# Where the right-hand tiles of a hybrid decoder layer begin: 64-byte steps in place of 32 past one

## The chip, the cores and the metric

The kernel runs on one core of one Trainium2 chip. The metric is the device time of one execution in microseconds (us). Three executions of the kernel before gave a median of 1153.29 us, from 1152.1 to 1153.56. A further execution was taken with the hardware profiler; every row of a profile below is from it.

## The reference, cut to what matters

One layer of a decoder on 1024 tokens of width 1024, all in float32:

```python
u = rms_norm(h, norm1_g)                       # (1024, 1024)
proj = u @ w_in                                # 3 x 512 for attention, 4 x 512 for the recurrence
attn = rms_norm(dilated_attention(aq, ak, av)) # 8 heads of 64, three dilations in one softmax
rec = hgrn2_mixer(hq, hf, hi, lb)              # 4 heads of 128, a gated linear recurrence in chunks
rec = rms_norm(rec) * silu(hg)
h = h + concat(attn, rec) @ w_out
u = rms_norm(h, norm2_g)
gate, val = split(u @ w_up)                    # 2 x 2816
h = h + (gelu(causal_conv3(gate)) * val) @ w_down
return rms_norm(h, final_norm_g)
```

## The kernel before, in words

**Products.** A float32 matrix product is made from three TensorE products. Each operand is split into a high part, rounded to the type fp32r, and a low part, what is left (`hi`, `lo`, on ScalarE and VectorE: the casts of line 88 and the subtractions of line 90 for the weights). The function `three` (lines 492 to 494) issues high by high, high by low and low by high into one PSUM bank; `prod` (lines 1233 to 1235) and the loop at lines 1532 to 1534 do the same in the channel mixer. Nearly all these matmuls have a stationary operand of 128x128 and a moving one of 128x512: a row of 2 KB in each partition. A smaller number of matmuls, in the attention and the recurrence and for sums over a row, work on plain float32 tiles, mostly 128x128 and smaller.

**Stages.** (1) The values of the attention and of the recurrence, V and I (PSUM tiles `v` and `i`), from the input x. Here x is the stationary operand and the weights move. (2) Queries and keys, and the recurrence's gates: `pair_block` computes a pair of heads with seven block products (PSUM tile `w`), in which the weights are stationary and x moves. These products also fill the gaps of the attention and of the recurrence, which are written out as steps: `scores`, `turn` and `values` of the attention, `recur` of the recurrence. The last pair of heads goes plainly (`phf`, `phq`). (3) The output projection (`po`). (4) The channel mixer: `w_up` (PSUM tiles `p0g`, `p0v`, `p1g`, `p1v` for the first two groups of columns, then `p`), the convolution, and `w_down` (`ds`, `da`, and `pdl` for the first two blocks of rows).

**Order.** The order of TensorE's instructions is the program's. That of the other engines is laid out by the framework's planner, apart from the instructions that the program pins. The weights go through a ring of five raw and five split buffers (`Ring`, pool `ring`).

**Where the tiles lie.** The on-chip memory (SBUF) is filled from two sides. Pools on the left stand one behind the other from its beginning; pools on the right are stacked from its end downwards, so each right-hand pool begins where the size of those above it puts it. A pool that is closed gives its room to the next.

| side | pools | tiles that matter here |
|---|---|---|
| left | `const`, `ring` | `vec`, `ones`, `lb`; the weights `raww`, `whi`, `wlo` |
| left | `ua` | x and its block sums T1, T3 and B22 for stages 1 and 2 |
| left | `hres`, `op`, `u20`, `u21` | h; the channel mixer's moving operands `b1`, `b12`, `b22`, T1 to T3 of stage 4 |
| left | `dx`, `dw`, `df`, `tail` | the operands of `w_down`: `fhi`, `flo`, `whi`, `wlo` |
| right | `eps` | the first right-hand pool: two constants, open all through |
| right | `ub` | x and its block sums B11, B21, T2 and T4 for stages 1 and 2; later in the same buffers (function `spare`) the operands `attn0`, `attn1`, `rec0`, `rec1` of `po` |
| right | `rv`, `at`, `xp`, `ab` | the identity for transposes; the attention's tiles |
| right | `hg` | the recurrence's tiles |
| right | `ff` | ten buffers of the channel mixer's activations (`atile`); also the split weights `ahiw`, `alow` of one block (stationary) and the split activations `ahi`, `alo` that `pdl` moves |

Tiles of 2 KB to 8 KB and the small ones of 64 bytes keep whatever place within 64 bytes the pool's start gave them. The names T1 to T4 and `whi`, `wlo` occur in two stages; in stages 1 and 2 the names are T1h, T1l and so on in rows of lines 492 to 494, in stage 4 in rows of lines 1233 to 1235.

The code that the diff touches, with the lines of the profile:

Of the kernel before, what the change touches and what calls it, by code (L numbers as in the profile page):

```python
# [10 lines left out]
F32 = mybir.dt.float32  # L11
# [6 lines left out]
P = 128  # L18
# [6 lines left out]
NG = 4  # L25
# [225 lines left out]
def hybrid_kernel(ctx: ExitStack, tc: tile.TileContext, xT, w_qk, w_tok, w_hg, w_out, w_up,  # L251
# [5 lines left out]
    def pool(name, side, **kw):  # L257
        return tc.tile_pool(name=name, bufs=1, side=side, reuse_waits="tile", **kw)
# [9 lines left out]

    lb = cpool.tile([P, 16], F32, name="lb")
    epool = ctx.enter_context(pool("eps", "right"))  # L270
    eps_ = epool.tile([P, 16], F32, name="eps")
    epst, onehalf = eps_[:, 0:1], eps_[:, 8:9]
    ub_cm = pool("ub", "right")
    ub = ub_cm.__enter__()
# [543 lines left out]
    with pool("hg", "right") as hg:  # L818
# [3 lines left out]
        def ht(tag, nm, bufs=1):  # L822
            return hg.tile([P, H2], F32, tag=tag, name=nm, bufs=bufs)
# [98 lines left out]


        lg = vec[:, V_LB : V_LB + 2 * NG]
        tm = hg.tile([P, NG], F32, name="lb_m")
        e01 = hg.tile([P, 2 * NG], F32, name="lb_e")
        DVE.tensor_tensor(tm, lg[:, 0:NG], lg[:, NG : 2 * NG], op=ALU.max)
        DVE.tensor_sub(e01[:, 0:NG], lg[:, 0:NG], tm)
        DVE.tensor_sub(e01[:, NG : 2 * NG], lg[:, NG : 2 * NG], tm)
# [23 lines left out]
        def recur(h, hf):  # L953
            A, E = (gate[h, hf].pop(x) for x in "AE")
            nm = f"{h}_{hf}"
# [6 lines left out]
            C = ht("C", "C" + nm)  # L962
            C3 = C.rearrange("p (c t) -> p c t", c=4)
            DVE.tensor_tensor_scan(C, chunks, A, 0.0, op0=ALU.mult, op1=ALU.add)
            ex = hg.tile([P, 12], F32, tag="ex", name=f"ex{nm}", bufs=2)
            order = tc.keep_in_program_order if (h, hf) == (3, 1) else lambda ins: ins
            A3 = A.rearrange("p (c t) -> p c t", c=4)
            DVE.tensor_sub(A3, C3, C3[:, :, 63:64].to_broadcast([P, 4, P]))
# [48 lines left out]
            for c in range(4):  # L1017
# [2 lines left out]
                PE.matmul(psO[:, s], AT[:, c], iv[:, c], start=True, stop=no_state)  # L1020
                if not no_state:
                    PE.matmul(psO[:, s], E[:, s], st[:, c], start=False, stop=True)
            sq, ss = ht("rs_m", f"hsq{nm}"), hg.tile([P, 12], F32, tag="sm", name=f"hss{nm}", bufs=2)
            for c in range(4):
                s = slice(c * P, (c + 1) * P)
                ACT.activation(sq[:, s], psO[:, s], AF.Square, accum_out=ss[:, c : c + 1])
# [37 lines left out]
        def rec_steps(h, hf):  # L1064
            chain = iter(())

            def first():
                nonlocal chain
                chain = recur(h, hf)
                next(chain)  # L1070

            yield first
            while True:
                yield lambda: next(chain, None)
# [559 lines left out]
```

## Time and profile before

| | |
|---|---|
| median of three executions | 1153.29 us (1152.1 to 1153.56) |
| profiled execution, its own time | 1153.45 us |
| its span, first to last instruction | 1151.7 us |
| mean granted clock of TensorE | 0.998 |
| TensorE matmul (PE) busy | 1138.9 us, 99% of the span, 6412 instructions |
| TensorE weight load (PEld) busy | 929.6 us, 81% |
| VectorE (DVE) busy | 960.3 us, 83% |
| ScalarE (ACT) busy | 586.8 us, 51% |
| GpSimd (POOL) busy | 87.8 us, 8% |
| DMA | 129.84 MB, mean 113 GB/s |

How to read the rows: `L493 PE MATMUL w<-T1l,whi` is the matmul of line 493 that writes the PSUM tile `w`; behind the arrow stands first the operand that moves, then the stationary one. Buffer numbers are left out. The time of a matmul in a row is from its start to its modelled end; matmuls overlap, so the next one begins before the end of the last, and "PE busy" holds such overlaps. The distance from one start to the next is the time that a matmul really takes of TensorE.

### The profile page before, as it was taken

The numbers are of one execution on the slowest core, as the hardware profiler recorded it, in microseconds if no ns is written. First come the engines' busy times: TensorE is split into PE (matmuls) and PEld (weight loads), VectorE is DVE, ScalarE is ACT, GpSimd is POOL, SyncE is SP. The second block draws the span as 40 slices with busy tenths as digits, with TensorE's granted clock in tenths as the row PEclk, the third lists the DMA queues.
The fourth block names the chain that finished last, engine by engine and source line by source line (L and its number), as shares of the span: only waits on it lengthen the run. The fifth ranks groups of instructions, "written<-read, shape, count | busy, mean of one in ns | idle before, by whom it ended". The sixth has DMA issues, their size and how long they took to land.

```text
span 1151.7 us, 17921 instructions
## 1 busy us (share of the span) xinstructions
PE 1138.9 (99%) x6412; PEld 929.6 (81%) x6412; DVE 960.3 (83%) x1748; ACT 586.8 (51%) x1177; POOL 87.8 (8%) x107
## 2 busy tenths in 40 slices
PE   9999999999999999999999999999999999999996
PEld 7887777778888888878788888888888888888885
DVE  7685877768999975889989989888988789857987
ACT  6444455556688875555434434343434354444553
POOL 5210233330000002000000000000000000000000
PEclk9999999999999999999999999999999999999999
DMA  7134222224313543321232233323332387435532
GB/s 249 46 111 145 61 72 62 84 82 159 110 56 110 156 128 103 99 65 38 72 116 98 92 118 125 105 73 111 128 103 80 111 269 230 123 101 171 158 118 75
DMA packets 98633, 129.84 MB, mean 113 GB/s; under 512 B 25008, under 2 KB 44240, under 8 KB 98544
## 3 DMA queue, kind: packets, MB, share of 16 engines
q1 hardware_dynamic: 84256, 104.03, 29.6%
q10 hardware_dynamic: 14288, 24.67, 5.7%
q8 instruction: 50, 0.82, 0.3%
q14 instruction: 39, 0.32, 0.1%
HBM read 97.58 MB, written 31.09 MB: 112 GB/s over the span
## 4 chain that ended last, share of the span: by engine, by line
PE 94%; DVE 3%; ACT 1%; DMA 1%; issue 0%; SPq 0%; ACTq 0%; DVEq 0%
PE p L1235 11%; PE p L1234 11%; PE p L1233 11%; PE w L492 5%; PE w L493 4%; PE w L494 4%; PE ds L1532 3%; PE ds L1533 3%; PE ds L1534 3%; PE po L492 3%; PE po L493 3%; PE po L494 2%; PE da L1533 2%; PE da L1532 2%; PE da L1534 2%; PE S L705 2%
## 5 line engine op out<-in xcount | busy, mean ns | idle before, releaser
L88 ACT CAST whi<-raww 128x512 fp32r<-128x512 f32 x257 | 157.6, 618 | 224.4 <-PE p L1234 78.1
L90 DVE TENSOR_TENSOR wlo<-raww,whi 128x512 fp32r<-128x512 f32 x258 | 179.7, 699 | 33.1 <-ACT whi L88 31.3
L88 ACT CAST whi<-r 128x512 fp32r<-128x512 f32 x70 | 43.6, 623 | 84.8 <-PE ds L1533 48.7
L90 DVE TENSOR_TENSOR wlo<-r,whi 128x512 fp32r<-128x512 f32 x70 | 47.8, 684 | 19.2 <-ACT whi L88 18.3
L1532 PE MATMUL ds<-fhi,whi 128*128 128x512 f32 x160 | 62.3, 389 | 0.0
L1533 PE MATMUL ds<-flo,whi 128*128 128x512 f32 x160 | 62.3, 389 | 0.0
L1534 PE MATMUL ds<-fhi,wlo 128*128 128x512 f32 x160 | 62.2, 389 | 0.0
L1233 PE MATMUL p<-b1h,whi 128*128 128x512 f32 x160 | 62.2, 389 | 0.0
L1234 PE MATMUL p<-b1l,whi 128*128 128x512 f32 x160 | 62.2, 389 | 0.0
L1235 PE MATMUL p<-b1h,wlo 128*128 128x512 f32 x160 | 62.2, 389 | 0.0
L718 POOL TENSOR_SCALAR P<-P,st 128x128 f32<-128x128 f32 (+7 forms) x64 | 45.5, 716 | 103.3 <-DVE st L717 94.4
L1506 POOL TENSOR_TENSOR facc<-facc,sqf 128x256 f32<-128x256 f32 x2 | 1.5, 738 | 674.4 <-ACT sqf L1505 674.4
L90 DVE TENSOR_TENSOR flo<-rawf,fhi 128x512 fp32r<-128x512 f32 x70 | 47.8, 683 | 3.2 <-ACT fhi L88 3.2
L88 ACT CAST fhi<-rawf 128x512 fp32r<-128x512 f32 x70 | 43.1, 616 | 13.5 <-PE p L1235 5.0
L716 ACT ACTIVATE P<-P,st 128x128 f32<-128x128 f32 (+7 forms) x64 | 35.7, 558 | 28.0 <-DVE st L714 28.0
L1262 ACT ACTIVATE cv<-cv 128x512 f32<-128x512 f32 x44 | 27.8, 632 | 40.3 <-DVE cv L1255 40.3
L1255 DVE SCALAR_TENSOR_TENSOR cv<-g,vec,cv 128x511 f32<-128x511 f32 (+2 forms) x92 | 44.6, 490 | 3.6 <-ACT cv L1252 3.3
L1532 PE MATMUL da<-fhi,whi 128*128 128x512 f32 x120 | 46.7, 389 | 0.0
L1533 PE MATMUL da<-flo,whi 128*128 128x512 f32 x120 | 46.7, 389 | 0.0
L1534 PE MATMUL da<-fhi,wlo 128*128 128x512 f32 x120 | 46.7, 389 | 0.0
L714 DVE CUSTOM_DVE_ANT_0 P<-S,mask 128x128 f32<-128x128 f32 (+7 forms) x64 | 28.9, 487 | 8.3 <-PE S L707 6.9
L1534 PEld LDWEIGHTS ds<-fhi,wlo 128*128 128x128 f32 x160 | 30.0, 188 | 6.3
(622 smaller groups left out, 3414.3 us busy)
## 6 DMA issues: line engine op xcount, KB each, us to landing
raww<-in_w_up_dram SPq DMA_DIRECT2D x88, 256.0 KB, 2.9
rawf<-spT SPq DMA_DIRECT2D x40, 256.0 KB, 2.8
r<-in_w_down_dram SPq DMA_DIRECT2D x40, 256.0 KB, 3.5
spB<-a ACTq DMA_DIRECT2D x30, 256.0 KB, 2.2
spT<-t ACTq DMA_DIRECT2D x30, 256.0 KB, 2.1
rawf<-spB SPq DMA_DIRECT2D x30, 256.0 KB, 2.7
raww<-in_w_out_dram SPq DMA_DIRECT2D x28, 256.0 KB, 2.8
raww<-in_w_hg_dram SPq DMA_DIRECT2D x24, 256.0 KB, 2.6
```

The source lines that it names most:

```text
L88: self.pin(self.high(hi[:, :w], raw))
L90: self.pin(low.tensor_sub(lo[:, :w], raw, f32(hi[:, :w])))
L492: PE.matmul(ps, a[0], b[0], start=start, stop=False)
L493: PE.matmul(ps, a[0], b[1], start=False, stop=False)
L494: PE.matmul(ps, a[1], b[0], start=False, stop=stop)
L718: POOL.tensor_scalar(Pt[:, :n], Pt[:, :n], st[:, 3:4], 1.0, op0=ALU.mult, op1=ALU.mult)
L1233: PE.matmul(ps, hi[:, s], bhi, start=(start and n == 0), stop=False)
L1234: PE.matmul(ps, hi[:, s], blo, start=False, stop=False)
L1235: PE.matmul(ps, lo[:, s], bhi, start=False, stop=(stop and n == len(rhs) - 1))
L1532: PE.matmul(ps[d], hi[:, s], ahi, start=(k == 0), stop=False)
L1533: PE.matmul(ps[d], hi[:, s], alo, start=False, stop=False)
L1534: PE.matmul(ps[d], lo[:, s], ahi, start=False, stop=(k == NPAIR - 1))
```

## The change

The constants' tile in the pool `eps` becomes 24 columns wide instead of 16 (96 bytes instead of 64 in each partition); the columns used, 0 to 15, stay the same. Four kinds of small tiles in the pool `hg` become 16 columns wide (64 bytes): `lb_m` (was 4), `lb_e` (was 8), `ex` and `hss` (were 12, two buffers each). The instructions use the same columns of them as before. All right-hand pools stand below `eps`, so their tiles begin 32 bytes lower; they begin at multiples of 64 bytes, where before they began 32 bytes past one.

```diff
@@ -268,7 +268,7 @@
     epool = ctx.enter_context(pool("eps", "right"))
-    eps_ = epool.tile([P, 16], F32, name="eps")
+    eps_ = epool.tile([P, 24], F32, name="eps")
     epst, onehalf = eps_[:, 0:1], eps_[:, 8:9]
@@ -922,8 +922,8 @@
         lg = vec[:, V_LB : V_LB + 2 * NG]
-        tm = hg.tile([P, NG], F32, name="lb_m")
-        e01 = hg.tile([P, 2 * NG], F32, name="lb_e")
+        tm = hg.tile([P, 16], F32, name="lb_m")[:, 0:NG]
+        e01 = hg.tile([P, 16], F32, name="lb_e")[:, 0 : 2 * NG]
@@ -962,7 +962,7 @@
-            ex = hg.tile([P, 12], F32, tag="ex", name=f"ex{nm}", bufs=2)
+            ex = hg.tile([P, 16], F32, tag="ex", name=f"ex{nm}", bufs=2)
@@ -1020,7 +1020,7 @@
-            sq, ss = ht("rs_m", f"hsq{nm}"), hg.tile([P, 12], F32, tag="sm", name=f"hss{nm}", bufs=2)
+            sq, ss = ht("rs_m", f"hsq{nm}"), hg.tile([P, 16], F32, tag="sm", name=f"hss{nm}", bufs=2)
```

## The prediction

> **What bounds the kernel now.** I read the page first: busy shares, slices, the chain of work that ended last.
>
> ```profile
> span 1151.7 us, 17921 instructions
> PE 1138.9 (99%) x6412; PEld 929.6 (81%) x6412; DVE 960.3 (83%) x1748; ACT 586.8 (51%) x1177; POOL 87.8 (8%) x107
> PE   9999999999999999999999999999999999999996
> PE 94%; DVE 3%; ACT 1%; DMA 1%; issue 0%; SPq 0%; ACTq 0%; DVEq 0%
> ```
>
> TensorE is busy in every slice and makes up 94% of the chain. A matmul's row overlaps the next matmul, though, so "busy" could hide stalls. The view in order of time gives the distance between starts, here in stage 1 and in the channel mixer:
>
> ```profile
> 30.11 0.40 PE L492 MATMUL v<-whi,B21h 128*128 128x512 f32 x1
> 30.34 0.39 PE L493 MATMUL v<-wlo,B21h 128*128 128x512 f32 x1
> ...
> 31.04 0.40 PE L493 MATMUL v<-wlo,B21h 128*128 128x512 f32 x1
> ...
> 600.16 0.39 PE L1235 MATMUL p<-b12h,wlo 128*128 128x512 f32 x1
> 600.38 0.39 PE L1233 MATMUL p<-b12h,whi 128*128 128x512 f32 x1
> ...
> 601.06 0.39 PE L1233 MATMUL p<-b12h,whi 128*128 128x512 f32 x1
> ```
>
> In the first group four starts take 0.93 us (30.11 to 31.04), 0.233 each; in the second four take 0.90 (600.16 to 601.06), 0.225 each. Both streams are dense. The difference lies in the matmuls, and the first stream's stationary operand B21 is a right-hand tile. The rows of one line with minimum, median and maximum show this cleanly:
>
> ```profile
> L493 PE MATMUL w<-B11l,whi x36: 391/396/403, 98.7 to 343.9; 128*128 128x512 f32 x36
> L493 PE MATMUL w<-T1l,whi x36: 387/389/397, 112.8 to 358.3; 128*128 128x512 f32 x36
> L493 PE MATMUL w<-T4l,whi x36: 392/395/403, 115.5 to 362.7; 128*128 128x512 f32 x36
> L493 PE MATMUL w<-B22l,whi x36: 387/389/398, 118.3 to 365.5; 128*128 128x512 f32 x36
> L493 PE MATMUL po<-attn0l,whi x32: 392/395/403, 394.3 to 436.1; 128*128 128x512 f32 x32
> L493 PE MATMUL po<-rec0l,whi x32: 392/395/403, 438.5 to 464.8; 128*128 128x512 f32 x32
> L493 PE MATMUL v<-wlo,T4h x16: 393/396/397, 10.7 to 29.6; 128*128 128x512 f32 x16
> L493 PE MATMUL v<-wlo,B22h x16: 389/389/389, 33.1 to 51.7; 128*128 128x512 f32 x16
> ```
>
> Same line, same stage, same weights, same shape: T1 and B22, on the left, have a median of 389 ns; B11, T4, `attn0` and `rec0`, on the right, 395 to 396. In stage 1, where x is stationary, the step is the same: 389 with B22, 396 with T4. So a right-hand operand on either side of the matmul costs about 6.5 ns (395.5 less 389).
>
> Is it the side or the start within 64 bytes? Stage 4 tells:
>
> ```profile
> L1235 PE MATMUL p<-T3h,wlo x80: 389/389/390, 555.8 to 917.7; 128*128 128x512 f32 x80
> L1234 PE MATMUL p1g<-b1l,ahiw 128*128 128x512 f32 x4 | 1.6, 395 | 0.0
> L1234 PE MATMUL p1g<-b1l,whi 128*128 128x512 f32 x4 | 1.6, 389 | 0.0
> L1463 PE MATMUL pdl<-ahi,w 128*128 128x512 f32 x16 | 6.3, 396 | 0.0
> ```
>
> The left pools of stage 4 hold 30 KB of ring, 32 of h, 12 of `op`, 32 of `u20` and 80 of `u21`, whose last tile is T3: it lies where `ub` lay earlier, and still takes 389. The stationary `ahiw` and the moving `ahi` in the right-hand pool `ff` take 395 and 396. High addresses are thus not slow; tiles of right-hand pools are, and what these share is the start 32 bytes past a multiple of 64.
>
> **The change part by part.** No instruction is added, removed or moved, none gets another shape, no transfer or wait is added; the wider tiles are used in the same columns. All that can change is what an access to a right-hand tile costs.
>
> *Matmuls of 512 columns.* With a moving right-hand operand: `w` with B11, B21, T2 and T4, 12 groups of 36, is 432; `po` with four operands, 12 groups of 32, is 384; `phf` and `phq`, 18 groups of 4, are 72; `pdl`, 3 groups of 16, are 48: 936. With a stationary one: `v` and `i` with B11, B21 and T4, 18 groups of 16, are 288; `ahiw` and `alow`, 6 groups of 4, are 24: 312. At 6.5 ns this is 6.1 and 2.0 us, together **8.1 us**.
>
> The 2.0 us rest on the stationary rows alone. The Trainium skill, page "TensorE: Matmul & The Clock Gate", Part 2, step 1, says that loading the next weights takes no read bandwidth from the running matmul, since the two have ports of their own. A reader who goes by that would give hidden weight loads no price and get 6.1 us in place of 8.1. The rows of T4h and B22h disagree: 396 against 389 with the same moving weights.
>
> *Matmuls of 256 columns and plain float32.*
>
> ```profile
> L1463 PE MATMUL pdl<-ahi,w 128*128 128x256 f32 x32 | 9.0, 281 | 0.0
> L372 PE MATMUL ssf<-facchi,ones 128*128 128x256 f32 x1 | 0.3, 282 | 0.0
> L1478 PE MATMUL ssf<-facc,ones x8: 378/379/483, 1139.8 to 1141.9; 128*128 128x256 f32 x8
> L458 PE MATMUL ss<-sums,ones 128*128 128x512 f32 x4 | 1.9, 592 | 0.0
> L733 PE MATMUL Tn<-ident,P 128*128 128x128 f32 x120 | 18.7, 275 | 0.0
> L997 PE MATMUL psU<-iv,kT 128*128 128x128 f32 x56 | 7.5, 274 | 0.0
> ```
>
> At 256 columns the right (`pdl`) takes 281 and the left (`facchi`) 282: nothing to gain in the other 96 matmuls of `pdl`. In plain float32, 512 moving right-hand columns take 592 and 256 left-hand ones 379: 213 ns for 256 columns. Going down the same slope, 128 columns would take 379 - 107 = 272, and the right-hand `psU` and `Tn` show 274 and 275. So I price them at zero; the upper end is 3 ns on some 420 such matmuls that follow one another (transposes 248, `psU` 56, `psO` 120), 1.3 us. Below zero nothing points.
>
> *Other engines and DMA.*
>
> ```profile
> L868 DVE TENSOR_TENSOR E<-E,R 128x512 f32<-128x512 f32 x4 | 2.7, 683 | 0.0
> L1382 DVE TENSOR_TENSOR v<-p,v 128x512 f32<-128x512 f32 x20 | 13.7, 683 | 2.0 <-PE p L1235 2.0
> L463 ACT CAST T2h<-x 128x512 fp32r<-128x512 f32 x4 | 2.5, 622 | 9.7 <-DVE x L479 6.9 <-DMA vd<-vt 2.8
> L1289 ACT CAST T2h<-uf 128x512 fp32r<-128x512 f32 x4 | 2.5, 620 | 1.2 <-DVE uf L1303 1.2
> ar<-raw SPq DMA_DIRECT2D x8, 256.0 KB, 2.8
> raww<-raw SPq DMA_DIRECT2D x8, 256.0 KB, 2.8
> ```
>
> VectorE takes 683 on a right-hand tile and on a left-hand one; ScalarE 622 and 620; the same DRAM tiles land in 2.8 us in the right-hand `ar` and in the left-hand `raww`. Zero for all three, with 2 ns per ScalarE instruction as the bound, off the path.
>
> *What of the 8.1 us reaches the end.* Where TensorE waits for others, a shorter matmul only lengthens the wait.
>
> ```profile
> 0.00:25.00 25.00, 23.67 (x91) 18.94 (x92) 17.42 (x20) 18.14 (x30) 12.29 (x14) 1.00 0.81 276
> 150.00:175.00 25.00, 25.00 (x332) 19.44 (x328) 17.50 (x51) 12.09 (x32) 7.42 (x12) 1.00 0.25 69
> 300.00:325.00 25.00, 25.00 (x139) 20.74 (x138) 24.74 (x46) 21.09 (x53) 2.16 (x1) 1.00 0.25 78
> 350.00:375.00 25.00, 25.00 (x134) 20.33 (x133) 23.03 (x41) 20.23 (x52) 0.29 (x1) 1.00 0.39 116
> PEld S L705 <- DVE st L717: 0.9, 3, 0.4
> ```
>
> (Columns of the first four rows: length, then busy time of PE, PEld, DVE, ACT and POOL, clock, DMA share, GB/s.) At the start x and the weights come in at 276 GB/s and TensorE waits; of the 91 matmuls there I write off the 48 with B11 in V: 48 by 6.5 ns, 0.3 us. In the attention (125 to 275 us) the longest named wait of the weight queue for another engine is 0.9 us, three times 0.3; shorter filling matmuls may give some of it back as waits: 0.2. In the recurrence VectorE is busy 24.74 of 25 us at 300 and 23.03 at 350, so it has 1 to 8% left; the right-hand matmuls of 512 columns there, counted by their starts, are 264 between 275 and 400 us, about 50 in 25 us, worth 0.3 us or 1.3%. It is late next, and I write off 0.5 us between 275 and 400. Sum: 8.1 - 0.3 - 0.2 - 0.5 = **7.1 us**, nearly all before 510 us, and 0.3 us from `pdl` at the end. The profiled execution took 1153.45 us with a span of 1151.7, close to the median of 1153.29; the span becomes 1144.6 and the median **1146.2**.
>
> **The rivals.**
>
> *No change.* The 6.5 ns come from something else about right-hand pools, and 1153.3 us stays. The Trainium skill, page "SBUF — State Buffer", Specifications (TRN2), gives 16-byte cachelines as what an access crosses; 32 past 64 is a whole number of these, so by that page no row would get shorter and the time would be this rival's. For the rival: no right-hand tile at a multiple of 64 exists in this trace. Against it: T3 at high addresses with 389, and VectorE, ScalarE and DMA, which don't tell the sides apart.
>
> *Moving operands only.* Stationary rows stay at 395: 8.1 - 2.0 = 6.1, less 0.8: 1148.0. Against it only that no other cause for those rows is in sight.
>
> *VectorE takes it back.* The recurrence goes at VectorE's pace and all 264 right-hand matmuls between 275 and 400 us give nothing: 1.7 instead of 0.5 us lost; the attention's, 193 by the same count, give nothing either, 1.3 instead of 0.2. 8.1 - 0.3 - 1.3 - 1.7 = 4.8: 1148.5. The digits of VectorE at 300 us speak for it; that TensorE's starts stay dense there, against.
>
> *More.* The float32 matmuls gain their 1.3 us and nothing is written off: 8.1 + 1.3, 1143.9.
>
> *Slower.* The planner lays out VectorE's queue from the tiles that it is given, four kinds of which change size. If it puts weight subtractions (699 ns each, rows of line 90 that write `wlo`) behind the recurrence's, TensorE starves between 275 and 450 us, as VectorE has no room there. Eleven such late ones, 7.7 us, eat the gain; from fourteen, 9.8 us, the kernel is slower by over 0.2%: 1156.0. Nothing in the diff changes a dependency or an instruction's size, so this is remote.
>
> ```profile
> L90 DVE TENSOR_TENSOR wlo<-raww,whi 128x512 fp32r<-128x512 f32 x258 | 179.7, 699 | 33.1 <-ACT whi L88 31.3 <-PE Tn L733 1.0
> ```
>
> **How the numbers follow.** Forecast 0.72; moving only 0.07; VectorE 0.07; more 0.04; no change 0.07; slower 0.03. What this kernel's measurement can tell from no change is about 0.2%, 2.3 us. Faster: 0.72 + 0.07 + 0.07 + 0.04 = 0.90; same 0.07; slower 0.03. The range goes from the "more" case, 1143.9, to just past the two reduced gains, 1149.0; no change and slower are left out.
>
> **What would show it.** Right: the rows `w<-B11l`, `w<-T4l`, `po<-attn0l`, `v<-wlo,T4h`, `p1g<-b1l,ahiw` and `pdl<-ahi,w` (512) at 389 beside unchanged T1 and B22; `pdl` at 256 columns still 281, `psU` 274, `ss` 592; the channel mixer beginning some 7 us earlier with the same length. Wrong: rows still at 395 (no change); `v` at 395 and `w` at 389 (moving only); rows at 389 with more idle time of the weight queue before 510 us (VectorE); left-hand rows that rise.

## The result, and the profile after

Over 22 executions each, the median went from 1152.22 us (1151.75 to 1153.67) to 1150.94 us (1150.59 to 1152.73): a ratio of 0.9987, 95% interval 0.9981 to 0.9993. The change makes the kernel faster by 1.3 us or 0.1%. The prediction was 1146.2 us, 7 us faster; the measured time lies outside its range, 1143.9 to 1149.0 us. The executions of each kernel fall into two groups some 1.7 us apart (near 1151.9 and 1153.5 us before, near 1150.8 and 1152.5 after); the median of three that the prediction started from and both profiled executions are of the second.

The page of the kernel after: the span, the busy times and the chain of work.

```profile
span 1150.6 us, 17921 instructions
PE 1137.8 (99%) x6412; PEld 930.4 (81%) x6412; DVE 959.7 (83%) x1748; ACT 587.0 (51%) x1177; POOL 88.2 (8%) x107
PE 94%; DVE 4%; ACT 1%; issue 1%; DMA 1%; ACTq 0%; SPq 0%; DVEq 0%
```

The bound is as before. The rows of line 493 that the prediction turned on, with minimum, median and maximum in ns, then first and last start in us (the rows of before stand in the prediction):

```profile
L493 PE MATMUL w<-B11l,whi x36: 389/394/400, 97.3 to 342.7; 128*128 128x512 f32 x36
L493 PE MATMUL w<-T1l,whi x36: 387/390/402, 111.4 to 357.2; 128*128 128x512 f32 x36
L493 PE MATMUL w<-T4l,whi x36: 388/395/399, 114.1 to 361.6; 128*128 128x512 f32 x36
L493 PE MATMUL po<-attn0l,whi x32: 388/394/399, 393.3 to 435.0; 128*128 128x512 f32 x32
```

Moving right-hand operands did not fall to 389. They begin at a multiple of 64 now, and still take 394 to 395 beside 390 for the left-hand T1. The groups of the same kernel in which a right-hand operand is stationary tell another tale (behind the bar the busy time in us and the mean of one in ns):

```profile
L1463 PE MATMUL pdl<-ahi,w 128*128 128x512 f32 x16 | 6.3, 395 | 0.0
L493 PE MATMUL v<-wlo,T4h 128*128 128x512 f32 x16 | 6.3, 394 | 0.0
L492 PE MATMUL v<-whi,T4h 128*128 128x512 f32 x16 | 6.3, 392 | 0.0
L494 PE MATMUL v<-whi,T4l 128*128 128x512 f32 x16 | 6.2, 388 | 0.0
```

With T4 stationary, three matmuls that all took 395 or so before now take 394, 392 and 388. The twelve such groups of V and I with T4 and B21 have a mean of 394.8 ns before and 391.7 after. From start to start, which is what counts, the matmuls of V and I with a right-hand operand take 233.2 ns before and 229.0 after, read from the differences of starts in the two traces. 288 of them by 4.2 ns are 1.2 us: the whole gain. The first-start column puts it in the same place: `w<-B11l` begins at 97.3 us instead of 98.7, 1.4 earlier, and `po<-attn0l` at 393.3 instead of 394.3, 1.0 earlier. Nothing is gained behind stage 1: the span is shorter by 1.1 us.

So the rows spoke against the cause that I had given them, but not for "no change" either. What tells stationary from moving operands?

### The profile page after: what moved, and what is told of

It reads as the page before. It is cut to its first block, busy times and chain, and to the rows that moved or that the text cites. A ratio compares the mean times of both kernels' runs of the same rounds, so it can differ in the third digit from the quotient of the medians.

```text
span 1150.6 us, 17921 instructions
## 1 busy us (share of the span) xinstructions
PE 1137.8 (99%) x6412; PEld 930.4 (81%) x6412; DVE 959.7 (83%) x1748; ACT 587.0 (51%) x1177; POOL 88.2 (8%) x107
## 4 chain that ended last, share of the span: by engine, by line
PE 94%; DVE 4%; ACT 1%; issue 1%; DMA 1%; ACTq 0%; SPq 0%; DVEq 0%
PE p L1235 11%; PE p L1234 11%; PE p L1233 11%; PE w L492 5%; PE w L494 5%; PE w L493 5%; PE ds L1532 3%; PE ds L1533 3%; PE ds L1534 3%; PE da L1532 2%; PE da L1533 2%; PE da L1534 2%; PE po L492 2%; PE po L493 2%; PE po L494 2%; PE S L705 2%
```

## Theories

In the program's allocation all left-hand operands, the ring of weights included, begin 192 bytes past a multiple of 512. Right-hand ones begin 416 past before and 384 past after; their slices are whole multiples of 512 further on. Three theories:

- **Multiple of 64**, the prediction's: a tile that begins 32 past a multiple of 64 is slow.
- **Place**: 192 past 512 is a good place by itself, others are bad.
- **Distance**: each matmul moves one operand while weights are loaded beside it. It is slow when the two begin at different places within some period (512 bytes or less). In the stream of V the load of the next weights starts some 3 ns after a matmul and takes 187 to 188 ns, less than the 227 to 235 ns to the next start, so it runs wholly beside that matmul. Left with left has distance 0. Right moving with left weights has 416 - 192 = 224 before and 192 after, and left moving with right weights the reverse.

## Experiments

Times are medians of several executions where a ratio is given. The others had one execution, which may lie anywhere in the 2 us over which this kernel scatters; there the rows carry the verdict. In the expectations "as after" means the kernel after the change.

### Equal starts

```diff
-    eps_ = epool.tile([P, 24], F32, name="eps")
+    eps_ = epool.tile([P, 72], F32, name="eps")
```

> The constants' tile is 72 columns wide instead of 24 (288 bytes): right-hand tiles begin 192 bytes past a multiple of 512, the same place within 512 bytes as all left-hand operands (before it was 416, after the change 384). Theory 'distance' (a matmul is slow when its moving row and the weights loaded meanwhile begin at different places within 512 bytes): all 1248 right-hand matmuls of 512 columns fall from 395 to 389 ns, in w, po, v, i and pdl, and the time to 1144 to 1146 us, 7 us under before. Theory 'multiple of 64' (the change's own): these tiles begin at a multiple of 64 as after the change, so rows and time are those of after, 1150.9 us. Theory 'place' (192 past 512 is good by itself): as 'distance'.

Measured: 1146.86 us, 0.9958 of before (0.9945 to 0.9972). Rows of line 493:

```profile
L493 PE MATMUL w<-B11l,whi x36: 387/389/398, 95.3 to 339.3; 128*128 128x512 f32 x36
L493 PE MATMUL w<-T1l,whi x36: 387/389/397, 109.2 to 353.6; 128*128 128x512 f32 x36
L493 PE MATMUL po<-attn0l,whi x32: 387/389/396, 389.3 to 430.4; 128*128 128x512 f32 x32
L493 PE MATMUL v<-wlo,T4h x16: 389/389/389, 9.1 to 27.5; 128*128 128x512 f32 x16
```

These tiles begin at multiples of 64 as after the change, yet all rows are at 389. "Multiple of 64" is out as the cause. The time is 5.1 us under the median of before in the same comparison (1151.94), a little short of what was expected.

### Both sides moved

```diff
-    lb = cpool.tile([P, 16], F32, name="lb")
+    lb = cpool.tile([P, 56], F32, name="lb")
-    eps_ = epool.tile([P, 24], F32, name="eps")
+    eps_ = epool.tile([P, 32], F32, name="eps")
```

> The left side moves up by 160 bytes (the tile lb is 56 columns wide), and the constants' tile on the right is 32 columns wide: operands of both sides begin 352 bytes past a multiple of 512, which is 32 past a multiple of 64. Theory 'distance': all matmuls of 512 columns at 389 ns, 1144 to 1146 us. Theory 'multiple of 64': everything now begins 32 past, so the right-hand rows are at 395 to 396 and the left-hand ones rise to it too: some 3100 more matmuls by 6 ns, about 1172 us. Theory 'place': neither side is at 192, so everything is slow, about 1172 us.

Measured: 1146.88 us, 0.9957 of before (0.9945 to 0.997). Groups:

```profile
L1235 PE MATMUL p<-T3h,wlo 128*128 128x512 f32 x80 | 31.1, 389 | 0.0
L493 PE MATMUL w<-B11l,whi 128*128 128x512 f32 x36 | 14.1, 390 | 0.0
L493 PE MATMUL po<-attn0l,whi 128*128 128x512 f32 x32 | 12.5, 389 | 0.0
```

Every operand begins 32 past a multiple of 64, and all matmuls are fast. Neither that start nor the place within 512 costs anything; "place" is out too. The time lies 0.9 us above the 1144 to 1146 that "distance" gave, as with equal starts.

### Weights apart from all other operands

```diff
     ringp = ctx.enter_context(pool("ring", "left"))
+    gap = ctx.enter_context(pool("gap", "left")).tile([P, 48], F32, name="gap")
     ...
     DVE.memset(ones, 1.0)
+    POOL.memset(gap, 0.0)
```

> The kernel after the change, with 192 unused bytes put on the left between the ring of weights and the pools behind it, so that the weights stay at 192 past a multiple of 512 and all other operands, left and right, begin at 384. Every tile begins at a multiple of 64. Theory 'distance': some 3012 matmuls that took 389 ns (w with T1, T3 and B22, and the channel mixer's p, p0, p1, ds and da) now have their moving row 192 from the weights and take about 395, as w with B11 does after the change: 3012 by 6.3 ns, 19 us more than after, 1167 to 1171 us; pdl at 512 columns and the matmuls with ahiw, whose two operands are now both at 384, fall to 389. Theory 'multiple of 64': rows and time of after, 1150.9 us. Theory 'own place of a tile': the time rises too, but pdl stays at 395.

Measured: 1168.5 us, 1.0145 of before (1.0129 to 1.0162). Two lines more make line 1235 the one of high by high, and 1465 the first of `pdl`. Groups:

```profile
L1534 PE MATMUL ds<-fhi,whi 128*128 128x512 f32 x160 | 63.2, 395 | 0.0
L1235 PE MATMUL p<-T3h,whi 128*128 128x512 f32 x80 | 31.6, 396 | 0.0
L495 PE MATMUL w<-T1l,whi 128*128 128x512 f32 x36 | 14.2, 395 | 0.0
L1465 PE MATMUL pdl<-ahi,w 128*128 128x512 f32 x16 | 6.2, 389 | 0.0
L1236 PE MATMUL p1g<-b1l,ahiw 128*128 128x512 f32 x4 | 1.6, 388 | 0.0
L1235 PE MATMUL p1g<-b1h,ahiw 128*128 128x512 f32 x4 | 1.6, 394 | 0.0
```

The channel mixer, fast in every other run, becomes slow with all tiles at multiples of 64, and `pdl`, whose operands are now in step (they begin at the same place within the period), becomes fast, 389 to 390. It costs 1168.5 - 1150.9 = 17.6 us against the kernel after; 19 were expected from 3012 matmuls. The theory of distance forecast the size and the larger exception. The other exception came only in part: the six small groups with `ahiw` and `alow`, in step too, stand at 388 to 394, 391.2 on average, where they had 391.5 after the change. They run in two stretches of twelve matmuls between out-of-step ones, and in each the first six or seven take 387 to 398 ns and the rest 388 or 389. What ran just before a matmul thus counts as well.

### The period: 128, 64, 256, 32 and 96 apart

One edit each, in the kernel after: 40, 56, 64 and 48 columns for the constants' tile instead of 24, and for 256 apart

```diff
-    eps_ = epool.tile([P, 24], F32, name="eps")
-    epst, onehalf = eps_[:, 0:1], eps_[:, 8:9]
+    eps_ = epool.tile([P, 8], F32, name="eps")
+    epst, onehalf = eps_[:, 0:1], eps_[:, 4:5]
...
-    DVE.memset(eps_[:, 0:8], EPS)
-    DVE.memset(eps_[:, 8:16], 1.5)
+    DVE.memset(eps_[:, 0:4], EPS)
+    DVE.memset(eps_[:, 4:8], 1.5)
```

> The constants' tile is 40 columns wide: right-hand tiles begin 320 past a multiple of 512, left-hand ones 192: 128 apart, both at multiples of 64. 'Distance' with a period of 512: rows of w and po still above 389, 392 to 395, time 1148 to 1152 us; with a period of 128: 389 and 1144 to 1146 us. 'Multiple of 64': as after the change, 1150.9 us, w at 395 and v between 388 and 395.

> The constants' tile is 56 columns wide: right-hand tiles begin 256 past a multiple of 512, left-hand ones 192: 64 apart. 'Distance' with a period of 512: w and po between 389 and 395, time 1146 to 1152 us; with a period of 64: 389 and 1144 to 1146 us, but then the change's 192 apart would have been fast already, which it was not. 'Multiple of 64': as after the change, 1150.9 us.

> The kernel after the change with the constants' tile 8 columns wide (32 bytes): right-hand tiles begin 448 past a multiple of 512, left-hand ones 192, so 256 apart, at multiples of 64. If the distance counts with a period of 256 or less: 389 ns everywhere and 1146 to 1147 us as with equal starts. If the period is 512 or more: w and po between 391 and 397, 1148 to 1153 us.

> The kernel after the change with the constants' tile 64 columns wide: right-hand tiles begin 224 past a multiple of 256 of which left-hand ones are 192 past, so the moving row of w and po lies 32 behind the weights' start and that of v and i 32 ahead, the reverse of before. If the price is a function of this distance alone, w and po take what v and i took before, 395 to 396, and v and i what w took, 395 to 396; pdl 395. Time 1151 to 1154 us. Theory 'nearly equal is good enough': 389 to 392 and 1147 to 1149 us.

> The kernel after the change with the constants' tile 48 columns wide: right-hand tiles begin 288 past a multiple of 512, left-hand ones 192, 96 apart. If the price is a function of the distance with a period of 256, w and po lie between what was measured 64 apart (390 to 392) and 128 apart (393 to 394); v and i, 96 the other way, at 395 to 396. Time 1150 to 1153 us.

Groups, each fence one kernel, 128, 64, 256, 32 and 96 apart in this order:

```profile
L493 PE MATMUL po<-attn0l,whi 128*128 128x512 f32 x32 | 12.6, 394 | 0.0
L493 PE MATMUL v<-wlo,T4h 128*128 128x512 f32 x16 | 6.3, 395 | 0.0
```

```profile
L493 PE MATMUL po<-attn0l,whi 128*128 128x512 f32 x32 | 12.5, 390 | 0.0
L493 PE MATMUL v<-wlo,T4h 128*128 128x512 f32 x16 | 6.3, 396 | 0.0
```

```profile
L493 PE MATMUL po<-attn0l,whi 128*128 128x512 f32 x32 | 12.5, 390 | 0.0
L493 PE MATMUL v<-wlo,T4h 128*128 128x512 f32 x16 | 6.2, 389 | 0.0
```

```profile
L493 PE MATMUL po<-attn0l,whi 128*128 128x512 f32 x32 | 12.6, 395 | 0.0
L493 PE MATMUL v<-wlo,T4h 128*128 128x512 f32 x16 | 6.3, 396 | 0.0
```

```profile
L493 PE MATMUL po<-attn0l,whi 128*128 128x512 f32 x32 | 12.7, 396 | 0.0
L493 PE MATMUL v<-wlo,T4h 128*128 128x512 f32 x16 | 6.4, 397 | 0.0
```

The times were 1153.37, 1149.93, 1146.82, 1152.26 and 1152.61 us. At 256 apart everything is as fast as with equal starts, so the period is 256 bytes or a divisor of it; 128 apart is slow, which rules out every smaller divisor. The time at 128 apart came out above the 1148 to 1152 expected; that one execution is within the scatter of before, and its rows are slow like those of before. At 96 apart `po` was expected between the values of 64 and 128 apart, 390 to 394, and took 395: the price doesn't rise evenly with the distance.

With the distance counted as start of the moving operand less start of the weights, within 256 bytes, the means in ns of groups of 512 columns fall on one table (averages of the whole numbers that the rows show). `po` is the mean of the four groups of line 493, where x moves; V and I is that of the twelve groups with T4 and B21, where the weights' buffers move and x is stationary:

| distance | 0 | +32 | +64 | +96 | 128 | -96 | -64 | -32 |
|---|---|---|---|---|---|---|---|---|
| `po` | 389.2 | 395.0 | 390.5 | 395.0 | 394.2 | | 395.5 | 395.5 |
| from | equal starts | 32 apart | 64 apart | 96 apart | 128 apart | | after | before |
| V and I | 389.0 | 394.8 | 391.7 | | 394.9 | 395.9 | 395.9 | 395.5 |
| from | equal starts | before | after | | 128 apart | 96 apart | 64 apart | 32 apart |

Two different stages, with the parts of the two sides exchanged, agree to 1.2 ns wherever both were measured. And the table holds the result of the change: the shift by 32 bytes took V and I from +32 (394.8) to +64 (391.7), the one cheap distance besides 0 among those run, and `po` and `w` from -32 to -64, where both cost 395.5.

### Whose weights

```diff
-        for t in order:
+        for t in order if c < KS else ():
     ...
+        for t in range(KS) if c >= KS else ():
+            for a, x in ((0, 0), (0, 1), (1, 0)):
+                for u in (t, t + KS):
+                    ...
+                    PE.matmul(banks[u], y[:, c % KS, tk], w[x], start=False, ...)
```

> The kernel before, with the matmuls of V and I reordered for the second half of x: a right-hand stationary tile (B21) and a left-hand one (B22) take turns, 96 matmuls of each, same work. It tells whose weights matter, the matmul's own or those loaded while it runs. If the next ones ('distance' between the moving row and the load that runs beside it): rows with B22 rise from 389 to 395 or 396, those with B21 fall from 395 to 389 to 391. If a matmul's own weights matter: B21 stays at 395 and B22 at 389. Time within 1 us of before either way.

Measured: 1155.0 us in one execution. Rows of V, taking turns:

```profile
L551 PE MATMUL v<-wlo,B22h x16: 396/396/397, 29.1 to 50.1; 128*128 128x512 f32 x16
L551 PE MATMUL v<-wlo,B21h x16: 394/394/395, 28.9 to 49.9; 128*128 128x512 f32 x16
```

B22, whose own weights are in step and whose next ones are not, rose from 389 to 396: the load that runs beside a matmul counts, as "distance" has it. B21 fell only to 394, not to the 389 to 391 expected, though the load beside it is in step. From start to start the two take 231.7 and 234.9 ns, as much together as two matmuls in a stream that is out of step throughout (233.2 each): taking turns saves nothing.

The trace before holds the same two cases, wherever a stretch with left-hand weights meets one with right-hand weights:

```profile
514.09 0.40 PE L1235 MATMUL p1g<-b1h,wlo 128*128 128x512 f32 x1
514.09 0.19 PEld L1233 LDWEIGHTS p1g<-b1h,ahiw 128*128 128x128 f32 x1
...
516.89 0.39 PE L1235 MATMUL p1g<-b1h,alow 128*128 128x512 f32 x1
516.89 0.19 PEld L1233 LDWEIGHTS p1g<-b12h,whi 128*128 128x128 f32 x1
```

The first of these matmuls has both operands on the left, and the load beside it is right-hand: it takes 396 ns. All 13 matmuls of that kind in V, I and `p1g` do. The second has right-hand weights of its own, and the load beside it is left-hand: it takes 389. Of the 15 of that kind, 5 take 389 and 10 take 393 or 394. So the load that runs beside the matmul counts each time, and a smaller part depends on what ran before. What carries that part over is not shown; the load's rows, 187 to 188 ns in all of this, don't show where the time goes.

The time missed its "within 1 us" by one or two. Of that, 96 rows of B22 by 7 ns explain 0.7. Paired start by start with the trace before, 2.6 us are lost between 98 and 111 us, behind the reordered matmuls: TensorE was busy 3.19 of the 5 us from 105 on (4.08 before) at a granted clock of 0.81 (1.00 before).

### The constants' tile alone

Only the first hunk of the change.

> Only the first part of the change: the constants' tile is 24 columns wide, the four small tiles of the pool hg stay as before. All theories: rows as after the change (w and po 395, v and i between 388 and 395), 1150 to 1153 us; the four small tiles are then worth nothing by themselves. If they matter, rows of the recurrence (psU, psO) differ from after by more than 2 ns.

Measured: 1150.8 us; `v<-whi,T4l` 392, `po<-attn0l` 394, and the recurrence's rows as after the change within 1 ns:

```profile
L997 PE MATMUL psU<-iv,kT 128*128 128x128 f32 x56 | 7.5, 274 | 0.0
```

By these rows and this one time, the four small tiles of `hg` are worth nothing.

### The version to keep

The kernel before with the constants' tile shrunk to 8 columns (the diff of "256 apart", from 16) and nothing else, which uses 32 bytes less instead of more.

> The kernel before with one edit: the constants' tile is 8 columns wide instead of 16 (32 bytes; columns 0 to 3 and 4 to 7 hold the two constants), so that right-hand tiles begin 448 past a multiple of 512, 256 from the left-hand ones; the small tiles of the pool hg stay. Theory 'distance with a period of 256': rows of w, po, v, i and pdl as with equal starts, 1146 to 1147.5 us, 0.995 to 0.996 of before. Theory 'the four small tiles matter': slower than the run with them by over 1 us.

Measured: 1146.68 us, 0.9952 of before (0.9939 to 0.9966). It beats both kernels. Its profiled execution began its stages with the data as late as that of before, so the first starts compare directly:

```profile
L493 PE MATMUL w<-B11l,whi x36: 387/389/398, 96.8 to 340.7; 128*128 128x512 f32 x36
L493 PE MATMUL po<-attn0l,whi x32: 387/389/396, 390.8 to 431.9; 128*128 128x512 f32 x32
L1235 PE MATMUL p<-T3h,wlo x80: 389/389/390, 550.8 to 912.8; 128*128 128x512 f32 x80
```

Against before, `w<-B11l` begins 1.9 us earlier (98.7), `po<-attn0l` 3.5 (394.3) and `p<-T3h,wlo` 5.0 (555.8): 1.9 us from V and I, 1.6 up to the output projection, 1.5 from there.

## Why the prediction was wrong, point by point

- **The bound and the price of a slow matmul: right.** TensorE's stream was dense, 6 to 6.5 ns per matmul was real, and it can be won: with equal starts all the groups named fell to 389.
- **The step that failed: "Is it the side or the start within 64 bytes?"** I excluded high addresses with T3 and then took the only property left, the start of the one operand. T3 shows more than I read from it: like every left-hand tile it lies in step with the weights that it meets. Each slow group had one operand from each side, each fast one both from one side, and I sorted the groups by an operand where I had to sort them by a pair. The doubly moved kernel (all 32 past 64, all fast) and the one with the weights apart (all at 64, the channel mixer slow) settle it. In place of the start within 64 bytes stands the distance from the weights: the change moved `w` and `po` from -32 to -64, both 395.5 ns. A matmul of the trace before spoke against my cause: `p1g<-b1h,wlo` at 514.09 us has both operands on the left and takes 396.
- **The stationary rows.** The 2.0 us that I set for them came as 1.2; the 6.1 us of moving rows came as nothing. The rival "moving only" had it the wrong way round. "No change" was nearest in time; it was right that the price comes from something else about right-hand tiles, and wrong that no row would get shorter (`v<-whi,T4l` went from 395 to 388).
- **The page's rule that I set aside.** The Trainium skill, page "TensorE: Matmul & The Clock Gate", Part 2, step 1, gives weight loads a read port of their own that takes nothing from the running matmul. The runs disagree where the two rows are out of step: where the weights loaded beside a matmul begin is then worth 6 ns in 233. Where they are in step, no row speaks against the page.
- **The rule behind "no change".** The 16-byte cachelines of the page "SBUF — State Buffer", Specifications (TRN2), in the Trainium skill were no guide to the time here: shifts by 32 bytes, two whole lines, do change rows, through the distance of two accesses and not through the start of one. No run tests the cachelines themselves.
- **Matmuls of 256 columns and plain float32: right.** `pdl` at 256 columns stayed at 279 to 284 in all kernels (281 before, 283 with equal starts), `psU` at 274 to 275.
- **What reaches the end: too much was counted.** The version to keep gains 5.1 us by medians where my sum, with the right cause, gives 7.1. Its matmuls run in the same order as before, so the distance from each start to the next can be compared one by one. Where it is at most 260 ns, so apart from waits, it fell by 6.2 ns in the right-hand matmuls of V and I, but only by 4.2 in those of `w` and by 5.1 in `po`, where I had priced all at 6.5, the step in the rows. By the number of matmuls that makes 1.8 us of the 2.8 priced for `w` and 2.0 of 2.5 for `po`. Why the starts close up less there than the rows shorten stays open. A wait that grew took another 0.5 us, behind the last matmul of `po` (the kernel before, then the version to keep; in brackets TensorE's idle time in us and what ended it):

```profile
500.11 0.47 PE L1233 MATMUL p0g<-b1h,whi 128*128 128x512 f32 x1 [0.23 <-DVE h L1128]
495.19 0.47 PE L1233 MATMUL p0g<-b1h,whi 128*128 128x512 f32 x1 [0.76 <-DVE h L1128]
```

- **VectorE as the next bound, and the planner.** VectorE took back this 0.5 us ahead of the channel mixer. In the recurrence, where I looked for it, the longest wait of the weight queue for VectorE grew only from 0.2 to 0.4 us (`E`, line 526). The planner's part did not appear: the order of every engine's instructions is the same in both kernels.

## What to carry to other kernels

When a row is slow for some operands and not for others, sort it by all operands that are read at that moment, the next weights included, before naming a cause; and before a change is costed on a cause, look for a row in which the cause is present and the effect is not. In streams of fp32r matmuls of 512 columns with new weights for each, as here, place the moving operands and the weights at the same offset modulo 256 bytes: in this kernel a shift of the right-hand tiles by 32 bytes is worth 0.5%, and 192 bytes at a wrong place cost 1.5%.

## What the runs showed of the hardware

The price of a matmul of 512 fp32r columns, 389 ns in step and up to 396 out of step (226.7 and 233.3 ns from start to start), depends on the distance, modulo 256 bytes, between the start of the moving row and that of the stationary tile that is loaded beside it, and hardly on where either lies. A smaller part depends on what ran just before. The price isn't symmetric: 64 one way costs 1 to 3 ns, 64 the other way 6 to 7. Why the memory acts so, which of the two reads waits, and whether distances that are no multiple of 32 are cheap, stays open.
